# A batched 64 x 64 matmul: block diagonals cleared by GpSimd, first b tiles on two queues, third a tile turned later

## The chip, the cores and the metric

The kernel runs on one core of one Trainium2 chip. A core has a matrix engine (TensorE, PE in the profile), a vector engine (VectorE, DVE), a scalar engine (ScalarE, ACT), GpSimd (POOL) and SyncE (SP). Each takes its own instructions in the order in which they were written and waits on semaphores for the others. Transfers between the chip's memory (HBM) and the on-chip memory (SBUF) are issued from SP, ACT or POOL, and carried out by 16 DMA engines. PE writes its products to PSUM, and another engine copies them to SBUF. The metric is the time of one execution in microseconds. A difference of 2% is about what a measurement of this kernel can tell from no change.

## What is computed

```python
def setup_inputs():
    return {
        "a": np.random.randn(1024, 64, 64).astype(np.float32),
        "b": np.random.randn(1024, 64, 64).astype(np.float32),
    }

def reference(a, b):
    return np.matmul(a, b).astype(np.float32)
```

There are 1024 independent products of 64 x 64 matrices. Each input has 16.8 MB and so has the output: 50.3 MB in all cross between HBM and SBUF.

## The kernel before

**Tiles.** A tile t is 64 products (16 tiles, `n_t`), and a step s is two tiles (8 steps, `n_s`). b is the moving operand of the matmul. a has to be turned first, since PE wants it with the inner dimension on the partitions. Four turned matrices are then laid on the diagonal of a 128-row operand that is zero elsewhere: the block diagonal, `at_bd0` and `at_bd1`, used in turn by even and odd tiles. Both are cleared once, at the start, one by DVE and one by GpSimd; later tiles write over the same diagonal places. Everything is computed in bf16. Two bf16 numbers are often moved as one fp32 word.

**Loads of a.** A step of a comes in four quarters h of 0.5 MB. The first step (`load_first_a`) is loaded as fp32, two quarters on SP's queue and two on ACT's, and is cast on ACT. Every later step (`load_a`) is loaded with three quarters cast to bf16 by the transfer itself, on POOL's queue (`cast_load_a`, tile `a_sb`), and the fourth as fp32 on SP's queue (tile `a_raw`). There are three buffers of each.

**Turning a.** Steps 0 and 1 (`ON_DVE`) are turned by DVE, one quarter at a time (`turn_a`), with the quarters that are still fp32 first cast by ACT. From step 2 on, `regroup` copies a step into one bf16 tile on DVE, `transpose` turns it on PE against an identity in two halves j, and ACT copies the results to `at_sb`. In all steps `spread` then copies the pieces to the block diagonal on DVE.

**b.** Tiles 0 to 3, 14 and 15 are loaded as fp32 (`load_b`, 1 MB each; the queue by `FIRST_B`, else SP) and cast by `cast`. Steps 2 to 6 (`PAIRS`) are loaded as a pair of tiles, in four transfers that cast to bf16 on POOL's queue (`load_pair`), and put in order by DVE (`turn`, one half per tile). All share three buffers (`b_sb`): a load waits until what was in its buffer has been cast or turned.

**Products.** `multiply` runs 64 matmuls per tile, in two halves with a PSUM tile `o_ps` each (two buffers). `evacuate` copies each half to `o_sb` in four copies, on ACT; in later odd tiles DVE does two of the second half's four. The result is stored one tile later (`HOLD`), in one transfer of 1 MB on POOL's queue; tile 14 goes in two, and tile 15 in four quarters on ACT's and SP's queues.

**Order.** The schedule is written by hand (`tc.manual_schedule()`): each engine runs its instructions in the order of the loop over t. In round t, `spread` and `cast` prepare tile t+1, `multiply` does tile t, then come the turning of later steps and the store of tile t-1. POOL's queue therefore mixes loads and stores in a fixed order, and each transfer on it waits for the one eight places earlier to be complete. For the start that order is a1, a2 (three casts each), the pair of step 2, a3, a4, the pair of step 3, the store of tile 0. The last load in it is a7, behind the store of tile 4.

The lines that matter: memsets 268 and 269, first loads 97, 105 and 76, casts 151, 154 and 197, DVE's turning of a 160, spreads 173 (steps 0 and 1) and 183, regroup 126 and 129, PE's transposes 138 with copies 141, pairs 111 and their turning 120, matmuls 241, evacuation 229, stores 218.

Of the kernel before, what the change touches and what calls it, by code (L numbers as in the profile page):

```python
# [8 lines left out]
fp32 = mybir.dt.float32  # L9
bf16 = mybir.dt.bfloat16  # L10
# [3 lines left out]
def kernel(  # L14
# [14 lines left out]
    nc = tc.nc  # L29
# [4 lines left out]
    n_t, n_s = B // 64, B // 128  # L34
    A_AHEAD = 3
# [2 lines left out]
    HOLD = 2  # L38
    PAIRS = (2, 3, 4, 5, 6)
    ON_DVE = (0, 1)  # L40
    FIRST_B = {0: nc.sync, 1: nc.sync, 2: nc.scalar, 3: nc.scalar}

    a_v = a.rearrange("(s g h) (mp v) k -> s h g mp (v k)", h=4, g=32, v=16)
    bp_v = b.rearrange("(s g h) k n -> s h g (k n)", h=4, g=32)
# [35 lines left out]

    def load_a(s, a_sb=None):
        a_sb = a_sb or cast_load_a(s)
        a_raw = a_pool.tile([128, 16, 64], fp32, name="a_raw")
        nc.sync.dma_start(out=a_raw[:].rearrange("p v k -> p (v k)"), in_=a_v[s, 3])
        a_tiles[s] = a_sb, a_raw

    def load_first_a():
# [34 lines left out]
    def regroup(s):  # L122
        a_sb = a_tiles.pop(s)
        a_bf = work.tile([128, 16, 4, 64], bf16, name="a_bf")
        cast_sb, raw = a_sb
        nc.vector.tensor_copy(  # L126
            a_bf[:, :, 0:3, :], cast_sb[:].rearrange("p h v k -> p v h k")
        )
        nc.vector.tensor_copy(a_bf[:, :, 3, :], raw[:])  # L129
        abf_tiles[s] = a_bf  # L130
        at_tiles[s] = work.tile([128, 32, 4, 4, 4], fp32, name="at_sb")

# [13 lines left out]
    def turn_a(s, h):  # L146
        if s == 0:
            if h == 0:
                abf_tiles[0] = work.tile([128, 16, 4, 64], bf16, name="a_bf")
            rows = abf_tiles[0][:, 4 * h : 4 * h + 4]  # L150
            nc.scalar.copy(rows.rearrange("p x y k -> p (x y k)"), a_tiles[0][h])  # L151
        elif h == 3:
            rows = work.tile([128, 16, 4, 64], bf16, name="a_bf")[:, 0:4]
            nc.scalar.copy(rows.rearrange("p x y k -> p (x y) k"), a_tiles[s][1][:])  # L154
        else:
            rows = a_tiles[s][0][:, h : h + 1]
        if h == 0:
            at_tiles[s] = work.tile([128, 4, 8, 4, 4, 4], fp32, name="at_sb")
        pairs = rows.rearrange("p x y k -> p (x y k)").bitcast(fp32)
        nc.vector.transpose(  # L160
            at_tiles[s][:, h].rearrange("p g w mp vo -> p w vo g mp"),
            pairs.rearrange("p (vo w kp) -> p w vo kp", vo=4, w=4),
        )

    def spread(t, hs=range(4)):
        bd = bd_tiles[t % N_BD]
        at_sb = at_tiles[t // 2]
        for h in hs:
            rows = slice(32 * h, 32 * h + 32)
            if t // 2 in ON_DVE:  # L170
                for i in range(2):
                    block = 32 * (2 * (t % 2) + i)
                    nc.vector.tensor_copy(  # L173
                        bd[rows, 8 * i : 8 * i + 8, :, h, :, :].rearrange(
                            "p g w mp vo -> p (g w) (mp vo)"
                        ),
                        at_sb[block : block + 32, h].rearrange(
                            "p g w mp vo -> p (g w) (mp vo)"
                        ),
                    )  # L180
            else:
                half = slice(16 * (t % 2), 16 * (t % 2) + 16)
                nc.vector.tensor_copy(  # L183
                    bd[rows, :, :, h, :, :].rearrange("p g w mp vo -> p (g w) (mp vo)"),
                    at_sb[rows, half].rearrange("p g w mp vo -> p (g w) (mp vo)"),
                )

    def cast(t):
        s, half = t // 2, t % 2
        if s in PAIRS:  # L190
            return
        if half == 0:
            bbf_tiles[s] = work.tile([128, 32, 128], bf16, name="b_bf")
        b_bf = bbf_tiles[s][:, 16 * half : 16 * half + 16]
        b_sb = b_tiles.pop(t)
        if t < n_t - 1:
            (nc.vector.tensor_copy if t > 1 else nc.scalar.copy)(b_bf, b_sb)  # L197
# [12 lines left out]
    def multiply(t):  # L210
        at_bd = bd_tiles[t % N_BD][:].rearrange("p g (j wl) h mp vo -> p j g (wl h mp vo)", j=2)
        at_bd = at_bd.bitcast(bf16).rearrange("p j g (c u) -> p j g c u", u=2)
        b_bf = bbf_tiles[t // 2][:, 16 * (t % 2) : 16 * (t % 2) + 16]
        last = t == n_t - 1
        o_sb = o_pool.tile([128, 8, 2, 2, 64], fp32, name="o_sb")

        def put(lo, n):
            store_queue(t, lo).dma_start(  # L218
                out=o_v[t, :, lo : lo + n, :],
                in_=o_sb[:, lo : lo + n].rearrange("p gh j wl n -> p (gh j wl n)"),  # L220
            )

        def evacuate(o_ps, gh, n, copies):

            for par in range(2):
                for wl in range(2):
                    src = o_ps[64 * wl : 64 * wl + 64, :, par, :, :]
                    dst = o_sb[64 * par : 64 * par + 64, gh : gh + n, :, wl, :]
                    copies[2 * par + wl](dst, src)  # L229

        for half in range(2):
            if not last:
                o_ps = o_psum.tile([128, 4, 2, 2, 64], fp32, name="o_ps")
            for g8 in range(8):
                if last and g8 % 4 == 0:
                    o_ps = t_psum.tile([128, 2, 2, 2, 64], fp32, name="at_ps")
                g = 8 * half + g8
                gl = (g8 % 4 if last else g8) // 2
                for j in range(2):
                    for u in range(2):  # L240
                        nc.tensor.matmul(  # L241
                            o_ps[:, gl, g % 2, j, :],
                            at_bd[:, j, g, :, u],
                            b_bf[:, g, 64 * u : 64 * u + 64],
                            start=(u == 0),
                            stop=(u == 1),
                        )
                if last and g8 % 4 == 3:
                    copy = nc.scalar.copy if g8 == 3 else nc.vector.tensor_copy
                    evacuate(o_ps, g // 4 * 2, 2, [copy] * 4)  # L250
            if not last:
                copies = [nc.scalar.copy] * 4
                if half and t % 2 and t > 6:
                    copies[2:] = [nc.vector.tensor_copy] * 2
                evacuate(o_ps, 4 * half, 4, copies)
        if last:
            held[t] = [lambda q=q: put(2 * q, 2) for q in range(4)]
        else:
            whole = t < n_t - 2
            held[t] = [lambda q=q: put(q, 8 if whole else 4) for q in ([0] if whole else [0, 4])]  # L260

    with tc.manual_schedule():
# [2 lines left out]
        nc.scalar.copy(warm[:, 1:2], warm[:, 0:1])  # L265
        load_b(0)
        load_b(1)
        nc.vector.memset(bd_tiles[0][:], 0.0)  # L268
        nc.gpsimd.memset(bd_tiles[1][:], 0.0)
        load_a(1)  # L270
        load_a(2)
        make_identity(nc, identity)
        for h in range(4):
            turn_a(0, h)
            spread(0, [h])
        cast(0)
        load_b(2)
        for t in range(n_t):
            s, half = t // 2, t % 2
            if t + 1 < n_t:  # L280
                spread(t + 1)
                cast(t + 1)
            if t == 0:
                load_b(3)
                load_pair(2)
            if t in (1, 2):
                load_pair(t + 2)
            if t in (8, 10):
                load_b(14 + (t - 8) // 2)
            if half == 0 and 0 < s < n_s - 1 - A_AHEAD:  # L290
                load_a(s + 1 + A_AHEAD)
            if half == 0 and 0 < s < n_s - 1:
                transpose(s + 1, 1)
            multiply(t)
            if t == 0:
                for h in range(4):
                    turn_a(1, h)
                a_tiles.pop(1)
                load_a(A_AHEAD)
                load_a(A_AHEAD + 1)  # L300
            if s + 1 in PAIRS:
                turn(s + 1, half)
                if half and 4 < s + 4 <= max(PAIRS):
                    load_pair(s + 4)
            if t == 1:
                regroup(2)
                transpose(2, 0)
            elif half == 0 and 0 < s and s + 2 < n_s:
                regroup(s + 2)
            elif half == 1 and s + 2 < n_s:  # L310
                transpose(s + 2, 0)
            if t >= HOLD - 1:
                store(t - HOLD + 1)
        for t in range(n_t - HOLD + 1, n_t):
# [31 lines left out]
```

## Time and profile before

| | us |
|---|---|
| median of 3 runs | 137.26 |
| lowest, highest | 135.27, 137.62 |
| the profiled execution | 136.3 |
| its span (first to last instruction) | 134.5 |

| engine | busy us | share of the span |
|---|---|---|
| DVE | 103.1 | 77% |
| ACT | 92.0 | 68% |
| PE | 66.9 | 50% |
| POOL | 46.0 | 34% |

| queue | MB written | share of 16 DMA engines |
|---|---|---|
| POOL's (q0) | 26.48 | 71.8% |
| SP's (q1) | 9.44 | 20.0% |
| ACT's (q10) | 3.67 | 8.0% |

The first numbers come from separate runs; everything else comes from the one profiled execution. Bytes of a queue are counted where they are written, so a load that casts to bf16 counts half of the fp32 that it reads. Line numbers are those of the kernel before; with the change the same functions stand some lines further down.

### The profile page before, as it was taken

What the parts mean: (1) busy time and instruction counts of PE and PEld (TensorE: products, weight loads), DVE (VectorE), ACT (ScalarE), POOL (GpSimd) and SP (SyncE); (2) the same over time, 40 slices, a digit from 0 to 9 for tenths busy, and PEclk for the clock granted to TensorE, in tenths of its full rate; (3) what the DMA queues carried; (4) which work ended last, traced back from release to release, by engine and by line L of the source; (5) the groups of instructions that cost most, each with busy time, mean ns of one, the idle gap of its engine ahead of it and who ended that gap; (6) DMA issues with size and microseconds to landing.
All of it is one profiled execution on the core that took longest, in us unless ns stands there. A gap on an engine that the chain in (4) does not pass through costs nothing.

```text
span 134.5 us, 2765 instructions
## 1 busy us (share of the span) xinstructions
PE 66.9 (50%) x1120; PEld 64.3 (48%) x1120; DVE 103.1 (77%) x133; ACT 92.0 (68%) x157; POOL 46.0 (34%) x64
## 2 busy tenths in 40 slices
PE   0000054055059667259936657674767475876400
PEld 0000054055059656259926657574757375866400
DVE  5699991006998999999998599989929999396900
ACT  3453140999715899999999909991898449999600
POOL 8940000391432374435345425363220020435000
PEclk9999999999999999965896777777775775555685
DMA  3999999999999999999999999999999999999991
GB/s 72 385 334 272 270 271 336 357 353 228 221 285 252 241 232 275 359 218 224 297 339 212 344 242 347 251 299 350 256 374 398 398 407 397 370 331 308 333 330 56
DMA packets 13932, 39.76 MB, mean 296 GB/s; under 512 B 1248, under 2 KB 2272, under 8 KB 13280
## 3 DMA queue, kind: packets, MB, share of 16 engines
q0 software_dynamic: 8080, 26.48, 71.8%
q1 hardware_dynamic: 3952, 9.44, 20.0%
q10 hardware_dynamic: 1888, 3.67, 8.0%
q8 instruction: 9, 0.15, 0.4%
q14 instruction: 3, 0.02, 0.0%
HBM read 33.55 MB, written 16.78 MB: 374 GB/s over the span
## 4 chain that ended last, share of the span: by engine, by line
DMA 65%; DVE 10%; ACT 7%; issue 5%; POOL 2%; PE 2%; SPq 2%; DVEq 0%; POOLq 0%
DMA b_sb<-in_b_dram 24%; DMA a_sb<-in_a_dram 23%; DMA out_dram<-o_sb 19%; ACT o_sb L229 5%; DVE at_bd L183 4%; DVE o_sb L229 4%; DVE b_bf L120 2%; POOL b_sb L111 1%; ACT b_bf L197 1%; PE at_ps L241 1%; SPq L105 1%; SPq L97 1%; PE o_ps L241 1%; POOL out_dram L218 0%; POOL a_sb L76 0%
## 5 line engine op out<-in xcount | busy, mean ns | idle before, releaser
L229 ACT COPY o_sb<-o_ps 64x512 f32<-64x512 f32 x112 | 65.0, 580 | 12.8 <-PE o_ps L241 11.2
L241 PEld LDWEIGHTS <-at_bd 128*128 128x128 bf16 x1024 | 47.9, 118 | 54.0 <-issue 36.2
L241 PE MATMUL o_ps<-b_bf,at_bd 128*128 128x64 bf16 x960 | 46.7, 222 | 50.7 <-ACT o_sb L229 22.6
L183 DVE COPY at_bd<-at_sb 32x1024 f32<-32x1024 f32 x48 | 34.2, 713 | 1.2
L218 POOL DMA_DIRECT2D out_dram<-o_sb x16 | 15.8, 990 | 36.5 <-issue 7.2
L120 DVE STREAM_TRANSPOSE b_bf<-b_sb 128x1024 f32<-128x1024 f32 x10 | 22.1, 2213 | 0.4 <-DMA b_sb<-in_b_dram 0.2
L138 PE MATMUL at_ps<-identity,a_bf 128*128 128x128 f32 x96 | 18.5, 374 | 7.2 <-DVE a_bf L129 7.2
L111 POOL DMA_DIRECT2D b_sb<-in_b_dram x20 | 12.0, 602 | 28.3 <-ACT b_bf L197 17.5
L138 PEld LDWEIGHTS at_ps<-identity,a_bf 128*128 128x128 f32 x96 | 16.9, 202 | 7.5 <-issue 6.6
L76 POOL DMA_DIRECT2D a_sb<-in_a_dram x21 | 14.0, 689 | 13.2 <-DMA b_sb<-in_b_dram 7.5
L141 ACT COPY at_sb<-at_ps 128x512 f32<-128x512 f32 x24 | 12.9, 596 | 5.6 <-PE at_ps L138 5.3
L160 DVE STREAM_TRANSPOSE at_sb<-a_bf 128x512 f32<-128x512 f32 x5 | 5.3, 1055 | 11.8 <-ACT a_bf L154 10.5
L173 DVE COPY at_bd<-at_sb 32x512 f32<-32x512 f32 x32 | 13.5, 423 | 0.7
L197 ACT CAST b_bf<-b_sb 128x2048 bf16<-128x2048 f32 x2 | 3.8, 1897 | 10.6 <-DMA b_sb<-in_b_dram 10.6
L229 DVE COPY o_sb<-o_ps 64x512 f32<-64x512 f32 x8 | 5.5, 689 | 4.8 <-ACT o_sb L229 4.7
L126 DVE COPY a_bf<-a_sb 128x3072 bf16<-128x3072 bf16 x6 | 5.8, 966 | 2.4 <-DMA a_sb<-in_a_dram 2.4
L151 ACT CAST a_bf<-o_sb 128x1024 bf16<-128x1024 f32 x4 | 4.1, 1044 | 3.2 <-DMA o_sb<-in_a_dram 3.2
L129 DVE CAST a_bf<-a_raw 128x1024 bf16<-128x1024 f32 x6 | 4.5, 746 | 0.0
L229 DVE COPY o_sb<-at_ps 64x256 f32<-64x256 f32 x8 | 3.4, 422 | 1.2 <-PE at_ps L241 1.1
L241 PE MATMUL at_ps<-b_bf,at_bd 128*128 128x64 bf16 x64 | 3.6, 242 | 1.2 <-DVE at_bd L183 1.2
L268 DVE MEMSET at_bd<- 128x4096 f32 x1 | 3.5, 3472 | 0.8 <-issue 0.8
L197 DVE CAST b_bf<-b_sb 128x2048 bf16<-128x2048 f32 x3 | 3.7, 1227 | 0.4 <-DMA b_sb<-in_b_dram 0.3
(16 smaller groups left out, 15.0 us busy)
## 6 DMA issues: line engine op xcount, KB each, us to landing
out_dram<-o_sb POOLq DMA_DIRECT2D x14, 1024.0 KB, 14.1
a_sb<-in_a_dram POOLq DMA_DIRECT2D x21, 256.0 KB, 13.6
b_sb<-in_b_dram POOLq DMA_DIRECT2D x20, 256.0 KB, 12.3
a_raw<-in_a_dram SPq DMA_DIRECT2D x7, 512.0 KB, 9.4
o_sb<-in_a_dram SPq DMA_DIRECT2D x2, 512.0 KB, 6.1
o_sb<-in_a_dram ACTq DMA_DIRECT2D x2, 512.0 KB, 6.9
out_dram<-o_sb POOLq DMA_DIRECT2D x2, 512.0 KB, 7.1
out_dram<-o_sb ACTq DMA_DIRECT2D x2, 256.0 KB, 6.3
```

Of the source, the lines that this page charges most:

```text
L76: nc.gpsimd.dma_start(out=a_sb[:, h, :, :].rearrange("p v k -> p (v k)"), in_=a_v[s, h], single_packet=True)
L111: nc.gpsimd.dma_start(out=pair[32 * h : 32 * h + 32, 0], in_=bp_v[s, h])
L120: nc.vector.transpose(cols[:, u], rows[:, u])
L126: nc.vector.tensor_copy(a_bf[:, :, 0:3, :], cast_sb[:].rearrange("p h v k -> p v h k"))
L138: nc.tensor.transpose(at_ps[:, vo, :], a_cols[:, 4 * vo + 2 * j + wl, :], identity[:])
L141: nc.scalar.copy(at_tiles[s][:, :, 2 * j + wl, :, :], at_ps[:].rearrange("p vo (g mp) -> p g mp vo", mp=4),)
L173: nc.vector.tensor_copy(bd[rows, 8 * i : 8 * i + 8, :, h, :, :].rearrange("p g w mp vo -> p (g w) (mp vo)"), at_sb[block : block + 32, h]. ...
L183: nc.vector.tensor_copy(bd[rows, :, :, h, :, :].rearrange("p g w mp vo -> p (g w) (mp vo)"), at_sb[rows, half].rearrange("p g w mp vo -> p ...
L197: (nc.vector.tensor_copy if t > 1 else nc.scalar.copy)(b_bf, b_sb)
L218: store_queue(t, lo).dma_start(out=o_v[t, :, lo : lo + n, :], in_=o_sb[:, lo : lo + n].rearrange("p gh j wl n -> p (gh j wl n)"),)
L229: copies[2 * par + wl](dst, src)
L241: nc.tensor.matmul(o_ps[:, gl, g % 2, j, :], at_bd[:, j, g, :, u], b_bf[:, g, 64 * u : 64 * u + 64], start=(u == 0), stop=(u == 1),)
```

## The change

The second memset moves from DVE to GpSimd, and both, with the identity, stand ahead of GpSimd's first load. b0 stays first on SP's queue, b1 moves to ACT's right behind ACT's two quarters of a0, and b2 moves up behind b0 on SP's. b3 comes on SP's queue, after cast 0, in place of ACT's after cast 1. The fourth quarter of a1 is loaded with a cast on POOL's queue, so ACT no longer casts it. Of ACT's work in the head, the cast of a0's first quarter and half of cast 0 go to DVE; of DVE's, the spread of quarter 2 of tile 0 goes to ACT. On POOL's queue a3 and a4 are loaded in rounds 0 and 1, which puts a4 behind the pair of step 3; the pair of step 5 comes one round earlier, ahead of the store of tile 1. Step 2 of a is turned on PE behind the matmuls of tile 2 (before: both halves ahead of them), and both halves of the pair of step 2 are put in order in round 2 (before: rounds 2 and 3); step 3 is regrouped in round 3 (before: round 2). DVE takes half of the second half's evacuation in tiles 12 and 14 too.

```diff
-    FIRST_B = {0: nc.sync, 1: nc.sync, 2: nc.scalar, 3: nc.scalar}
+    FIRST_B = {1: nc.scalar}
...
     def load_a(s, a_sb=None):
         a_sb = a_sb or cast_load_a(s)
-        a_raw = a_pool.tile([128, 16, 64], fp32, name="a_raw")
-        nc.sync.dma_start(out=a_raw[:].rearrange("p v k -> p (v k)"), in_=a_v[s, 3])
+        a_raw = a_pool.tile([128, 16, 64], fp32, name="a_raw")[:].rearrange("p v k -> p (v k)")
+        if s in ON_DVE:
+            a_raw = a_raw.bitcast(bf16)[:, 0:1024]
+            nc.gpsimd.dma_start(out=a_raw, in_=a_v[s, 3], single_packet=True)
+        else:
+            nc.sync.dma_start(out=a_raw, in_=a_v[s, 3])
         a_tiles[s] = a_sb, a_raw
...
-            rows = abf_tiles[0][:, 4 * h : 4 * h + 4]
-            nc.scalar.copy(rows.rearrange("p x y k -> p (x y k)"), a_tiles[0][h])
+            rows = abf_tiles[0][:, 4 * h : 4 * h + 4].rearrange("p x y k -> p (x y k)")
+            (nc.scalar.copy if h else nc.vector.tensor_copy)(rows, a_tiles[0][h])
         elif h == 3:
-            rows = work.tile([128, 16, 4, 64], bf16, name="a_bf")[:, 0:4]
-            nc.scalar.copy(rows.rearrange("p x y k -> p (x y) k"), a_tiles[s][1][:])
+            rows = a_tiles[s][1]
...
-    def spread(t, hs=range(4)):
+    def spread(t, hs=range(4), copy=nc.vector.tensor_copy):
...
-        if t < n_t - 1:
+        if t == 0:
+            nc.scalar.copy(b_bf[:, 0:8], b_sb[:, 0:8])
+            nc.vector.tensor_copy(b_bf[:, 8:16], b_sb[:, 8:16])
+        elif t < n_t - 1:
             (nc.vector.tensor_copy if t > 1 else nc.scalar.copy)(b_bf, b_sb)
...
-                if half and t % 2 and t > 6:
+                if half and (t % 2 and t > 6 or t > 11):
                     copies[2:] = [nc.vector.tensor_copy] * 2
...
         load_b(0)
         load_b(1)
-        nc.vector.memset(bd_tiles[0][:], 0.0)
-        nc.gpsimd.memset(bd_tiles[1][:], 0.0)
+        load_b(2)
+        for bd in bd_tiles:
+            nc.gpsimd.memset(bd[:], 0.0)
+        make_identity(nc, identity)
         load_a(1)
         load_a(2)
-        make_identity(nc, identity)
-        for h in range(4):
-            turn_a(0, h)
-            spread(0, [h])
+        turn_a(0, 0)
+        spread(0, [0])
+        turn_a(0, 1)
+        spread(0, [1])
+        turn_a(0, 2)
+        turn_a(0, 3)
+        spread(0, [2], nc.scalar.copy)
+        spread(0, [3])
         cast(0)
-        load_b(2)
+        load_b(3)
         for t in range(n_t):
...
-            if t == 0:
-                load_b(3)
-                load_pair(2)
-            if t in (1, 2):
+            if t < 3:
                 load_pair(t + 2)
+                load_a(t + A_AHEAD) if t < 2 else None
...
-            if half == 0 and 0 < s < n_s - 1:
+            if half == 0 and 1 < s < n_s - 1:
                 transpose(s + 1, 1)
             multiply(t)
             if t == 0:
                 for h in range(4):
                     turn_a(1, h)
                 a_tiles.pop(1)
-                load_a(A_AHEAD)
-                load_a(A_AHEAD + 1)
-            if s + 1 in PAIRS:
-                turn(s + 1, half)
-                if half and 4 < s + 4 <= max(PAIRS):
-                    load_pair(s + 4)
-            if t == 1:
+            elif t == 1:
                 regroup(2)
+            elif t == 2:
                 transpose(2, 0)
-            elif half == 0 and 0 < s and s + 2 < n_s:
-                regroup(s + 2)
-            elif half == 1 and s + 2 < n_s:
-                transpose(s + 2, 0)
+                transpose(2, 1)
+                turn(2, 0)
+                turn(2, 1)
+                load_pair(5)
+            elif t == 3:
+                regroup(3)
+                transpose(3, 0)
+            else:
+                if s + 1 in PAIRS:
+                    turn(s + 1, half)
+                    if half and s + 4 <= max(PAIRS):
+                        load_pair(s + 4)
+                if half == 0 and s + 2 < n_s:
+                    regroup(s + 2)
+                elif half == 1 and s + 2 < n_s:
+                    transpose(s + 2, 0)
             if t >= HOLD - 1:
                 store(t - HOLD + 1)
```

More of the change, by code (lines that the diff above doesn't have):

```diff
@@ L128, in regroup @@
         )
-        nc.vector.tensor_copy(a_bf[:, :, 3, :], raw[:])
+        nc.vector.tensor_copy(a_bf[:, :, 3, :], raw.rearrange("p (v k) -> p v k", v=16))
         abf_tiles[s] = a_bf
@@ L149, in turn_a @@
                 abf_tiles[0] = work.tile([128, 16, 4, 64], bf16, name="a_bf")
-            rows = abf_tiles[0][:, 4 * h : 4 * h + 4]
-            nc.scalar.copy(rows.rearrange("p x y k -> p (x y k)"), a_tiles[0][h])
+            rows = abf_tiles[0][:, 4 * h : 4 * h + 4].rearrange("p x y k -> p (x y k)")
+            (nc.scalar.copy if h else nc.vector.tensor_copy)(rows, a_tiles[0][h])
         elif h == 3:
-            rows = work.tile([128, 16, 4, 64], bf16, name="a_bf")[:, 0:4]
-            nc.scalar.copy(rows.rearrange("p x y k -> p (x y) k"), a_tiles[s][1][:])
+            rows = a_tiles[s][1]
         else:
-            rows = a_tiles[s][0][:, h : h + 1]
+            rows = a_tiles[s][0][:, h].rearrange("p v k -> p (v k)")
         if h == 0:
             at_tiles[s] = work.tile([128, 4, 8, 4, 4, 4], fp32, name="at_sb")
-        pairs = rows.rearrange("p x y k -> p (x y k)").bitcast(fp32)
+        pairs = rows.bitcast(fp32)
         nc.vector.transpose(
@@ L172, in spread @@
                     block = 32 * (2 * (t % 2) + i)
-                    nc.vector.tensor_copy(
+                    copy(
                         bd[rows, 8 * i : 8 * i + 8, :, h, :, :].rearrange(
```

## The prediction

> **What bounds the kernel now.** First the page's DMA row and its HBM line.
>
> ```profile
> DMA  3999999999999999999999999999999999999991
> HBM read 33.55 MB, written 16.78 MB: 374 GB/s over the span
> ```
>
> The transfer engines are busy from 3 us to the end, while no compute engine passes 77%. The change moves the same 50.33 MB. So I ask at what rate they cross, by stretch, and then what the last stores wait for. The windows give the rate (start:end, length, the engines' busy times, granted clock, DMA share, GB/s):
>
> ```profile
> 4.00:8.00 4.00, 0.00 (x0) 0.00 (x0) 2.72 (x3) 2.09 (x2) 3.92 (x9) 1.00 1.03 416
> 8.00:20.00 12.00, 1.74 (x34) 1.85 (x35) 11.56 (x22) 3.89 (x4) 0.23 (x1) 1.00 1.09 273
> 20.00:28.00 8.00, 1.93 (x38) 1.82 (x36) 0.83 (x1) 4.34 (x7) 2.23 (x5) 1.00 1.05 348
> 28.00:40.00 12.00, 5.00 (x71) 4.75 (x71) 8.37 (x16) 8.11 (x14) 5.30 (x8) 1.00 1.05 264
> 100.00:115.00 15.00, 10.26 (x153) 9.76 (x151) 14.40 (x18) 10.66 (x19) 1.97 (x3) 0.61 1.03 399
> 115.00:130.00 15.00, 8.41 (x149) 7.85 (x146) 9.02 (x17) 11.29 (x23) 4.17 (x4) 0.61 0.97 332
> ```
>
> GB/s counts bytes written; a load that casts fp32 to bf16 reads twice that. By the queue table of the same stretches POOL's queue (casts only, until 40 us) wrote 1.51 MB in 8 to 20, 0.06 in 20 to 28 and 1.35 in 28 to 40. With these doubled, HBM moved 398, 355 and 375 GB/s there. Full pace is about 400, and it is missed in two places: 20 to 40 us moved 7.34 MB where 8.0 could pass (1.65 us lost), and 115 to 130 us 4.95 where 6.0 could (2.6 us).
>
> The timeline of the head (start, length, engine, line; in brackets the idle time before and what ended it):
>
> ```profile
> 16.31 1.90 ACT L197 CAST b_bf<-b_sb 128x2048 bf16<-128x2048 f32 x1 [5.20 <-DMA b_sb<-in_b_dram]
> 18.26 3.57 PE L241 MATMUL o_ps<-b_bf,at_bd 128*128 128x64 bf16 x64 [18.26 <-ACT b_bf L197]
> 23.58 1.90 ACT L197 CAST b_bf<-b_sb 128x2048 bf16<-128x2048 f32 x1 [5.37 <-DMA b_sb<-in_b_dram]
> 25.77 2.00 POOL L111 DMA_DIRECT2D b_sb<-in_b_dram  x4 [17.54 <-ACT b_bf L197]
> ```
>
> Tile 0's multiplication waits for b0 (landed 16.3), and POOL stands still for 17.5 us until b1 is cast and its buffer free. That hole is the slow stretch: in 20 to 28 us only SP's and ACT's queues move bytes.
>
> The timeline of the tail:
>
> ```profile
> 100.18 1.13 DVE L126 COPY a_bf<-a_sb 128x3072 bf16<-128x3072 bf16 x1 [2.40 <-DMA a_sb<-in_a_dram]
> ...
> 114.21 1.23 DVE L197 CAST b_bf<-b_sb 128x2048 bf16<-128x2048 f32 x1
> ...
> 117.78 1.39 DVE L229 COPY o_sb<-o_ps 64x512 f32<-64x512 f32 x2 [2.34 <-ACT o_sb L229]
> ...
> 119.20 3.09 DVE L183 COPY at_bd<-at_sb 32x1024 f32<-32x1024 f32 x4
> ...
> 122.34 3.44 PEld L241 LDWEIGHTS <-at_bd 128*128 128x128 bf16 x64 [1.33 <-DVE at_bd L183]
> ```
>
> From the landing of the last a tile (a7) at 100.1 us the work runs through DVE in its issue order: regroup, spread 12, evacuation of 11, turn of b, spreads 13 and 14, cast 14, evacuation of 13, spread 15, tile 15. DVE ends at 127.8 and the last stores land some 5 us later. So the end is set by (a) when a7 lands, which is a matter of bytes ahead of it, and (b) the chain behind it.
>
> **The change, part by part.**
>
> *GpSimd.* The second memset (3.51, row L269) and the identity (0.30 + 0.35) go ahead of POOL's loads: the first issue moves from 4.19 to 8.35 us. In before nothing of that queue moved until after 8 us, 4 us behind its issue, so I expect its first bytes near 12.5. Cover: the a0 loads (2.1 MB) and b0, b1, b2 (1.05 MB each) are on SP and ACT by then, 5.2 MB or 13 us at 400 GB/s from 2.4 us on. Cost 0; without the cover up to 4.2 us. a1's fourth quarter becomes a POOL cast, one issue more (0.57) ahead of pair 2: the seven end at 12.3, before cast 1 (about 17) lets pair 2 go.
>
> *DVE and ACT in the head.* DVE loses its memset (3.47), which lay beside the wait for a0. One cast of a0 goes from ACT (1.04) to DVE (nearest row L129, 0.75). Two spreads go from DVE (0.42) to ACT, unseen there: between 0.58 (row L229, 512 elements) and 1.04 (row L151, 1024 from SBUF), I take 0.65. All of it is beside the wait for b0. Cast 0 is halved between both engines: 1.90 becomes 1.0.
>
> *b on both queues.* b0 leads SP's queue, b1 leads ACT's right behind a0, b2 follows on SP. a0, b0 and b1 are 4.2 MB, 10.5 us at 400: b0 and b1 land near 14 to 14.5 (16.3 and 23.6 before). Multiplication 0 starts near 15.5 (18.3), cast 1 ends near 17, pair 2 is issued then (25.8), and POOL's queue has no hole. a1 needs no ACT cast, so DVE's 10.5 us wait for it goes: a1 is turned by about 24 (32.3). b2 lands near 21, multiplication 2 starts near 28.5, no longer queued on PE behind the transposes of a2 (42.0 before). b3 is now on SP, behind b2 and the raw quarter of a2 and ahead of the raw quarter of a3: beside pair loads that queue had 0.73 MB in 28 to 40, so b3 lands at 36 (42.3 at worst, as before). Four tiles are ahead by 8 to 13 us, and then DVE, busy 19.13 of 20 us in 40 to 60, absorbs most: multiplication 4 waits for spread 4, regroup 3 and the transposes of a3, near 50 (52.6).
>
> *What of it reaches the end.* a7 is the last load in POOL's order, with the same five stores ahead of it as before. Its landing moves only by the better rate. If the hole is gone, 20 to 40 us gains between 0 and 1.65 us. The early stretch of b0 beside b1 on the two queues resembles the 355 row, and could give back 5 us x 45 GB/s = 0.23 MB, 0.55 us. I take half of the gain, 0.8.
>
> *Tail.* Evacuation of the second halves of tiles 12 and 14 moves half to DVE: four ACT copies less (4 x 0.58), four DVE copies more (4 x 0.69 = 2.76). In DVE's order from 106.1: turn 2.2, spread 13 2.8, two copies 1.4 (new), spread 14 2.85, cast 14 1.23: 116.6. There DVE used to wait 2.34 us for ACT's evacuation of tile 13, up to 117.78. ACT has two copies less ahead of it, and o_ps is free earlier, so DVE goes straight on: copies to 118.0, spread 15 to 121.0 (122.3 before), cast 15 0.83, two copies (new) 1.4 to 123.2, while PE starts tile 15 at once. DVE's last copy ends near 126.6 in place of 127.8: 1.15 us. DMA has room in 115 to 130.
>
> Sum: 0.8 + 1.15 = 1.95. The profiled execution took 136.3 us (span 134.5 and 1.8 around it): 134.35. The median shown is 137.26, 0.96 above it; I put the forecast between, at 134.8.
>
> **Rivals.** *No change, 136.0 to 137.3.* The head is hidden whole, because bytes bound it. First, 0.63 MB of b15 still crossed after a7 (SP's queue in 100 to 115); issued earlier and ahead of a7 they delay it by 1.6 us, which leaves 0.35 of the sum. Second, the rate may not depend on which queues are filled: the rows of 398 and 355 differ in the kinds of packets too; then the 0.8 goes and the sum is 135.15. Third, DVE's early copies may not run beside GpSimd's longer memsets: two spreads beside the identity's took 1.00 where 0.85 is usual. If the first cast waits from 5.3 to 7.8, 2.4 us of the 2.6 us lead at tile 4 are gone. Against all three: DVE's 2.34 us wait in the tail is real.
>
> The Trainium skill (DMA: Bandwidth & Descriptors, section "Issuing engines are not separate DMA queues") states the second as a rule: all issuing engines' DMAs run on the same 16 engines, and spreading them saves only issue time. The Trainium skill (SBUF — State Buffer, section "Who interferes with whom") states the third: a DVE copy in a two-port mode and a GpSimd instruction exclude each other for a whole instruction. The rows before the change agree with both, and prove neither.
>
> *Both losses recovered, 132.1.* 1.65 + 2.6 = 4.2 us off 136.3. For: in 120 to 125 us the DMA share is 0.91, so the stores come late. Against: the chain behind a7 shortens by 1.15 only.
>
> *Slower, 139 to 141.* DVE becomes the tail's bound. Its 2.76 us of new copies wait in order, and pay nothing back where PE's second half of tile 12 or 14 isn't ready: each such wait holds spread 14 or the last copies. It decides once DVE's idle 2.34 us is gone, which the first two copies and one wait of 1 us use up; then all 2.76 stand at the end, 139.1, or 140.0 on the median, and more with waits. For: DVE is 14.40 of 15 us busy in 100 to 115. Against: PE ends tile 12 by 111, when spread 13 ends.
>
> **How the numbers follow.** Forecast 0.45 (own range 133.3 to 136), no change 0.22, both recovered 0.17, slower 0.16. Two per cent of the median, 2.75 us, is about what runs that spread from 135.27 to 137.62 can tell: under 134.5 is faster, over 140 slower. Half of the forecast's case and all of the third are faster: 0.39. Two thirds of the slower case pass 140: 0.11. The rest is 0.50. The range leaves out the far side of the last two cases: 132 to 138.8.
>
> **What would show it.** Right: PE's first multiplication at 15 to 16.5 us, pair 2 issued near 17, and no stretch under 390 GB/s of HBM traffic between 20 and 40. a7's landing at 98 to 100; DVE going from cast 14 to the copies of tile 13 with under 0.5 us between; its last copy 1 us or more closer to that landing than 27.7. Wrong: the same a7 landing with a filled hole (bytes, the second case); DVE's last copy later behind a7 (the fourth); or slow DMA between 8 and 13 us, with GpSimd's loads late and no cover.

## The result and the profile after

The changed kernel takes 137.61 us (median of 20 runs, 136.40 to 138.86) beside 136.15 (20 runs, 135.12 to 137.62) for the kernel before on the same chip: a ratio of 1.0109, 95% interval 1.0079 to 1.0138. It is slower by 1.1%. With 20 runs of each kernel the interval reaches 0.3% to either side, so differences well under the 2% named at the start can be told. The prediction was 134.8 with a range of 132.0 to 138.8: the range holds the time, the sign is wrong. The profiled execution took 137.22 us, with a span of 135.4 (before 136.3 and 134.5).

The page of the changed kernel, its DMA row and its HBM line:

```profile
DMA  3999999999999999999999999999999999984993
HBM read 33.55 MB, written 16.78 MB: 372 GB/s over the span
```

The hole is now near the end: a slice at 40%, where before every slice but the first and the last was full. The windows of the changed kernel (start:end, length, busy time of PE, PEld, DVE, ACT and POOL, granted clock, DMA share, GB/s written):

```profile
8.00:16.00 8.00, 0.00 (x0) 0.10 (x1) 7.07 (x11) 3.22 (x4) 4.65 (x8) 1.00 1.06 299
...
100.00:115.00 15.00, 8.13 (x112) 7.74 (x112) 11.67 (x15) 7.24 (x13) 0.89 (x1) 0.66 1.03 394
115.00:130.00 15.00, 9.06 (x160) 8.61 (x160) 14.46 (x24) 9.98 (x21) 4.23 (x4) 0.55 0.83 286
120.00:124.00 4.00, 3.47 (x64) 3.31 (x63) 3.86 (x6) 2.16 (x4) 1.36 (x1) 0.50 0.47 170
```

The last of these stretches, in the kernel before:

```profile
120.00:124.00 4.00, 2.83 (x55) 2.67 (x53) 3.06 (x5) 3.86 (x8) 2.36 (x3) 0.50 0.89 314
```

In 120 to 124 us the transfer engines have half of their time free (a share of 0.47, before 0.89): the stores come too late to fill it. That is the tail. The head shows in the queues of 8 to 16 us (packets, MB written, share of 16 engines), in the changed kernel:

```profile
q10 hardware_dynamic: 536, 1.09, 45.2%
q1 hardware_dynamic: 530, 1.05, 44.8%
q0 software_dynamic: 122, 0.25, 16.4%
```

and in the kernel before:

```profile
q0 software_dynamic: 536, 1.00, 65.9%
q1 hardware_dynamic: 563, 1.12, 40.4%
q10 hardware_dynamic: 34, 0.07, 2.4%
```

With POOL's casts (q0) counted twice, as they read twice what they write, HBM moved 1.09 + 1.05 + 0.50 = 2.64 MB in these 8 us, or 330 GB/s, beside 1.12 + 0.07 + 2.00 = 3.19 MB, or 399, before. In both the engines are occupied all the time (the shares add up to more than 100%). In 20 to 40 us it is the other way: 5.46 MB written, of which 2.68 by casts, make 8.14 MB or 407 GB/s, where 7.34 MB moved before. So the slow stretch was not filled but moved, from 20-40 us to 8-16. What is left over is small: by the packets of the trace 14.40 MB had crossed at 40 us, beside 14.12 before, 0.28 MB or 0.7 us at 400 GB/s.

Nothing of that shows at a7, whose regroup starts at 100.63 us (100.18 before). In 100 to 116 us SP's queue carried 0.31 MB, beside 0.63 before: 0.32 MB more of b15 had crossed ahead of a7. In all, 39.1 MB had crossed when a7 was there, 38.7 before.

Behind a7, DVE's timeline in the changed kernel:

```profile
108.47 3.16 DVE L186 COPY at_bd<-at_sb 32x1024 f32<-32x1024 f32 x4
114.05 1.39 DVE L235 COPY o_sb<-o_ps 64x512 f32<-64x512 f32 x2 [2.42 <-ACT o_sb L235]
115.47 3.09 DVE L186 COPY at_bd<-at_sb 32x1024 f32<-32x1024 f32 x4
118.59 1.23 DVE L203 CAST b_bf<-b_sb 128x2048 bf16<-128x2048 f32 x1
119.85 1.39 DVE L235 COPY o_sb<-o_ps 64x512 f32<-64x512 f32 x2
121.28 3.09 DVE L186 COPY at_bd<-at_sb 32x1024 f32<-32x1024 f32 x4
```

Spread 13 ends at 111.63, 11.0 us behind the start of the last regroup, as before. Then DVE waits 2.42 us for ACT, and only after that come the two new copies of tile 12 (114.05) and spread 14 (115.47). The wait of 2.34 us that stood behind cast 14 is gone, as forecast, but one of 2.42 us now stands ahead of the new copies. DVE waits for ACT as long as before, so the copies that were to fill this wait come on top of it: counted from the start of the last regroup, spread 14 ends 3.9 us later than before and spread 15 still 1.6 us later. PE's timeline in the changed kernel, and the start of tile 14 in the kernel before:

```profile
112.87 1.09 PE L247 MATMUL o_ps<-b_bf,at_bd 128*128 128x64 bf16 x32 [0.94 <-ACT o_sb L235]
115.59 1.87 PE L247 MATMUL o_ps<-b_bf,at_bd 128*128 128x64 bf16 x32 [1.62 <-DVE o_sb L235]
119.88 3.59 PE L247 MATMUL o_ps<-b_bf,at_bd 128*128 128x64 bf16 x64 [2.42 <-DVE b_bf L203]
```

```profile
116.60 1.87 PE L241 MATMUL o_ps<-b_bf,at_bd 128*128 128x64 bf16 x32 [0.51 <-ACT o_sb L229]
```

Of the changed kernel, the first two rows are the halves of tile 13, the third is tile 14. Its start is 3.3 us later than before, and the second half of tile 13 waits 1.62 us for DVE's new copies to free `o_ps`. DVE's last copy ends 29.75 us behind the start of the last regroup, 27.58 before. The last transfer ends at 133.92, 0.83 later than before (133.09): of the 2.2 us in the chain more than half is taken back, for the last store is through 3.5 us behind DVE's last copy, where it took 5.3. That the emptier queues are the reason was not tested.

### The profile page after: what moved, and what is told of

The parts are those of the page before. It is cut to its first block, busy times and chain, and to the rows that moved or that the text cites. A ratio compares the mean times of both kernels' runs of the same rounds, so it can differ in the third digit from the quotient of the medians.

```text
span 135.4 us, 2775 instructions
## 1 busy us (share of the span) xinstructions
PE 65.2 (48%) x1120; PEld 62.2 (46%) x1120; DVE 106.0 (78%) x136; ACT 88.0 (65%) x152; POOL 49.2 (36%) x66
## 4 chain that ended last, share of the span: by engine, by line
DMA 63%; DVE 13%; issue 6%; POOL 6%; PE 5%; ACT 2%; DVEq 0%; POOLq 0%
DMA b_sb<-in_b_dram 28%; DMA a_sb<-in_a_dram 23%; DMA out_dram<-o_sb 11%; DVE o_sb L235 5%; PE o_ps L247 5%; DVE at_bd L186 4%; POOL at_bd L276 3%; ACT o_sb L235 2%; POOL a_sb L76 2%; DVE b_bf L124 2%; DVE b_bf L203 1%; DVE b_bf L208 1%; DVE a_bf L133 1%; POOL identity masks.py:199 0%; POOL a_raw L86 0%
## 5 line engine op out<-in xcount | busy, mean ns | idle before, releaser
L235 ACT COPY o_sb<-o_ps 64x512 f32<-64x512 f32 x108 | 62.7, 580 | 21.0 <-PE o_ps L247 19.6
L142 PE MATMUL at_ps<-identity,a_bf 128*128 128x128 f32 x96 | 16.6, 345 | 10.1 <-DVE a_bf L133 10.1
L76 POOL DMA_DIRECT2D a_sb<-in_a_dram x21 | 13.4, 645 | 18.4 <-DMA a_sb<-in_a_dram 12.2
L142 PEld LDWEIGHTS at_ps<-identity,a_bf 128*128 128x128 f32 x96 | 15.0, 184 | 10.3 <-issue 6.0
L176 DVE COPY at_bd<-at_sb 32x512 f32<-32x512 f32 x30 | 12.7, 423 | 0.8
L235 DVE COPY o_sb<-o_ps 64x512 f32<-64x512 f32 x12 | 8.3, 690 | 4.3 <-ACT o_sb L235 4.2
L276 POOL MEMSET at_bd<- 128x4096 f32 x2 | 7.0, 3512 | 0.3 <-POOLq L347 0.3
L155 DVE CAST a_bf<-o_sb 128x1024 bf16<-128x1024 f32 x1 | 3.4, 3418 | 4.1 <-DMA o_sb<-in_a_dram 4.1
L155 ACT CAST a_bf<-o_sb 128x1024 bf16<-128x1024 f32 x3 | 3.0, 1043 | 3.7 <-DMA o_sb<-in_a_dram 3.7
L163 DVE STREAM_TRANSPOSE at_sb<-a_bf 128x512 f32<-128x512 f32 x4 | 4.0, 1045 | 0.1
```

The costliest lines, as they stand in the source:

```text
L76: nc.gpsimd.dma_start(out=a_sb[:, h, :, :].rearrange("p v k -> p (v k)"), in_=a_v[s, h], single_packet=True)
L142: nc.tensor.transpose(at_ps[:, vo, :], a_cols[:, 4 * vo + 2 * j + wl, :], identity[:])
L155: (nc.scalar.copy if h else nc.vector.tensor_copy)(rows, a_tiles[0][h])
L176: copy(bd[rows, 8 * i : 8 * i + 8, :, h, :, :].rearrange("p g w mp vo -> p (g w) (mp vo)"), at_sb[block : block + 32, h].rearrange("p g w ...
L276: nc.gpsimd.memset(bd[:], 0.0)
```

## The experiments

Two causes stand against each other. **Head theory:** both memsets and the identity ahead of POOL's first load leave 8 to 16 us without casts, and bytes not moved there are paid for at the end. **Tail theory:** the copies of tiles 12 and 14 given to DVE wait for ACT and hold spread 14 up. All ratios are to the kernel before on the same chip; every row of the table is from one profiled execution except the ratio. These columns vary: e5 and e16 are the same kernel, and their last regroups start at 100.01 and 97.75. Small differences between two traces therefore say little.

| kernel | ratio, 95% interval | last regroup starts | DVE's last copy ends | last transfer ends |
|---|---|---|---|---|
| before | 1 | 100.18 | 127.76 | 133.09 |
| the change | 1.0109 [1.0079, 1.0138] | 100.63 | 130.38 | 133.92 |
| e1 tail undone | 1.0019 [0.9988, 1.0049] | 101.22 | 128.67 | 133.03 |
| e2 tail alone | 1.0042 [1.0010, 1.0075] | 101.00 | 130.27 | 133.96 |
| e3 tile 14 only | 1.0061 [1.0022, 1.0099] | 100.91 | 129.41 | 133.40 |
| e4 tile 12 only | 1.0171 [1.0134, 1.0208] | 101.69 | 130.82 | 135.09 |
| e5 e1, memsets split | 0.9942 [0.9908, 0.9977] | 100.01 | 128.19 | 132.56 |
| e6 e1, b1 on SP | 1.0023 [0.9985, 1.0061] | 100.73 | 128.92 | 133.28 |
| e8 DVE's copies first | 1.0069 [1.0028, 1.0110] | 101.02 | 129.23 | 133.21 |
| e10 e5, b14, b15 on POOL | 0.9959 [0.9911, 1.0008] | 96.27 | 124.77 | 131.47 |
| e12 change, memsets split | 0.9958 [0.9920, 0.9996] | 98.76 | 128.54 | 132.42 |

**e1 and e2: the tail rule, taken out and put in alone.** e1 is the change without it, e2 the kernel before with it.

```diff
-                if half and (t % 2 and t > 6 or t > 11):
+                if half and t % 2 and t > 6:
```

> The changed kernel with the evacuation of tiles 12 and 14 as it was before (all four copies of the second half on ACT); the head stays changed. Tail theory: in the changed kernel DVE stood 2.42 us for ACT's first copies of tile 12 before its own two, with spread 14 queued behind them, so DVE ended 29.8 us behind a7's landing where 27.7 was usual. Without the rule it ends 27.7 us behind a landing near 100.5, and the time is that of the kernel before: ratio 0.998 to 1.003. Rival, head theory (slow transfers in 8 to 16 us and late GpSimd loads cost the time): the ratio stays 1.008 to 1.014.

> The kernel before with only the new evacuation rule for tiles 12 and 14. Tail theory: DVE stands about 2.4 us ahead of its copies of tile 12, ends 2 us later behind a7, and the ratio is 1.009 to 1.016. Head theory: no change, 0.998 to 1.002.

Without the rule the change's loss falls from 1.1% to an interval that holds 1: 0.9% belong to the rule. Alone, on the old head, it costs 0.4%. That is less than the 0.9 to 1.6% expected, although DVE's wait (1.96 us) and the longer chain (29.3 us from the last regroup to DVE's last copy) are there too; so what the rule costs depends on the rest of the kernel. DVE's timeline in e1:

```profile
109.06 6.02 DVE L186 COPY at_bd<-at_sb 32x1024 f32<-32x1024 f32 x8
115.11 1.23 DVE L203 CAST b_bf<-b_sb 128x2048 bf16<-128x2048 f32 x1
118.68 1.39 DVE L235 COPY o_sb<-o_ps 64x512 f32<-64x512 f32 x2 [2.35 <-ACT o_sb L235]
```

Spreads 13 and 14 stand in one piece again and end at 115.1, where the change ends them at 118.6; the wait for ACT is back behind cast 14, ahead of spread 15 alone. e1 also shows that the change's head alone, with all that it reorders, gains nothing measurable (1.0019, the interval holds 1).

**e3 and e4: one tile of the rule at a time.**

```diff
-                if half and (t % 2 and t > 6 or t > 11):
+                if half and (t % 2 and t > 6 or t > 13):    (e3)
+                if half and (t % 2 and t > 6 or t == 12):   (e4)
```

> The changed kernel with the new evacuation for tile 14 alone. Tail theory: no wait ahead of spread 14; the two copies of tile 14 stand ahead of DVE's last eight, which wait for tile 15's matmuls anyway, so they cost 0.6 us at most: ratio 1.000 to 1.006. If the cost were DVE's added busy time (4 copies of 0.69) and no wait, half of it would stay: 1.005 to 1.008. Head theory: 1.008 to 1.014.

> The changed kernel with the new evacuation for tile 12 alone. Tail theory: the wait of 2.4 us ahead of DVE's copies stays, and nearly the whole loss with it: ratio 1.006 to 1.012. Busy-time theory: half of the loss, 1.004 to 1.007. Head theory: 1.008 to 1.014.

Tile 12 is the costly one, as the place of the wait says. The ratio of e3 (1.0061) lies at the end of the range of its tail theory and inside that of the busy-time theory, so it does not decide between them. That tile 12 alone cost more than both tiles together (1.0171 beside 1.0109, the intervals just touching, with five timed runs) was not foreseen, and no run settles it. In its one trace the chain is not the longer one (29.1 us behind the last regroup, 29.75 in the change); the regroup itself starts 1.1 us later.

**e8: the same copies, but the first two of a half in place of the last two.**

```diff
-                if half and (t % 2 and t > 6 or t > 11):
+                if half and t % 2 and t > 6:
                     copies[2:] = [nc.vector.tensor_copy] * 2
+                if half and t in (12, 14):
+                    copies[:2] = [nc.vector.tensor_copy] * 2
```

> The changed kernel, with DVE doing the first two copies of the second half in tiles 12 and 14, and ACT the last two. Same number of copies on each engine. If DVE's wait of 2.42 us is for ACT's copies of the same tile, it shrinks to the end of PE's second half (0.3 to 0.6 us), spread 14 comes 2 us sooner and the ratio is 1.001 to 1.006. If the copies cost by their busy time alone, nothing changes: 1.008 to 1.014.

This tells whether DVE had waited for PE or for ACT. DVE's timeline in e8:

```profile
112.57 1.39 DVE L235 COPY o_sb<-o_ps 64x512 f32<-64x512 f32 x2 [0.55 <-PE o_ps L247]
113.99 3.09 DVE L186 COPY at_bd<-at_sb 32x1024 f32<-32x1024 f32 x4
```

And who kept ACT waiting in the same kernel (releaser, us, times), from the view of the tile `o_sb`:

```profile
  PE o_ps L247: 17.0, 8
  DVE o_sb L235: 4.0, 2
```

DVE's wait falls from 2.42 to 0.55 us, and now PE ends it. Spread 14 starts 1.5 us earlier than in the change. In exchange ACT waits 4.0 us for DVE, in two waits, for which the change's trace has no such entry: the four copies of one half run one engine after the other in this program, whichever comes first. So DVE's wait in the change was for ACT's two copies of the same half, which end there at 114.02, and not for the product. The time (1.0069) lies between the change and e1, in neither of the two ranges expected, and its interval overlaps the change's: the trace decides this, not the time.

**e5 and e12: the memsets split again.** DVE clears one block diagonal and POOL the other, POOL's casts are issued right behind that, and the identity comes after them. e5 has the old tail rule, e12 the change's.

```diff
-        for bd in bd_tiles:
-            nc.gpsimd.memset(bd[:], 0.0)
-        make_identity(nc, identity)
+        nc.vector.memset(bd_tiles[0][:], 0.0)
+        nc.gpsimd.memset(bd_tiles[1][:], 0.0)
         load_a(1)
         load_a(2)
+        make_identity(nc, identity)
```

> The changed kernel with the old evacuation rule (as e1_tail_undone), and with the clearing shared again: DVE clears the first block diagonal, GpSimd the second, and GpSimd's loads go ahead of the identity. Cover theory: without casts in flight the loads of b0 and b1 run at 315 to 345 GB/s in 8 to 16 us, where 400 is usual; with the casts 4.2 us earlier these 8 us move 0.5 MB more, DVE's first cast takes 0.7 us in place of 3.42, and the ratio falls from 1.002 to 0.988 to 0.996. Rival (what is gained in the head goes to loads of b that cross ahead of a7, and the end doesn't move): 0.998 to 1.004.

> The whole change, evacuation of tiles 12 and 14 included, with the clearing alone shared between DVE and GpSimd as before, and GpSimd's loads ahead of the identity. If the two costs add (1.0109 with both; 1.0019 without the tail; 0.9942 without either), this is 1.001 to 1.006. If one hides the other, it stays at 1.008 to 1.013 or falls under 0.998.

With the old rule the ratio goes from 1.0019 to 0.9942, with the change's from 1.0109 to 0.9958. Everything else of the head is untouched, so 0.8 to 1.5% belong to these lines: one memset back on DVE, and the identity behind POOL's casts. Which of the two matters more was not tried; both let POOL's first issue come at 4.19 us again, not 8.48. e12 also came out under 0.998, where the sum of the two costs would have given 1.001 to 1.006: they do not simply add.

The gain can be followed to a7. At 40 us, 14.03 to 14.12 MB have crossed in the traces with the old head, 14.32 to 14.40 with the change's and 14.78 to 14.97 with the mended one (the memsets split). In the eight traces in which POOL clears both block diagonals (the change, e1, e3, e4, e6, e8, e13, e14), the last packet of a7 comes at 100.1 to 101.2 us; in the four with the memsets split and b as in the change (e5, e12, e15, e16) and in e9, the same up to there, at 97.3 to 99.5; in the three with the old head (before, e2, e7) at 99.7 to 100.9. So the change's head does not bring a7 forward, and the mended one does.

**e6: b1 on SP's queue behind b0, not on ACT's.**

```diff
-    FIRST_B = {1: nc.scalar}
+    FIRST_B = {}
```

> The changed kernel with the old evacuation rule (as e1_tail_undone), and b1 on SP's queue behind b0, so that ACT's queue is empty after a0. If the slow 8 to 16 us come from two queues of b's 512-byte pieces side by side, HBM moves over 380 GB/s there with one queue; if they come from the missing casts, it stays at 315 to 345. b1 lands some 4 us later. Ratio 0.998 to 1.006 by either, for the end follows a7.

The rival for the slow 8 to 16 us is that two queues of b disturb each other. The queues of that stretch in e6:

```profile
q1 hardware_dynamic: 975, 1.96, 83.7%
q0 software_dynamic: 168, 0.31, 20.5%
q10 hardware_dynamic: 30, 0.07, 2.1%
```

They move 1.96 + 0.07 + 0.62 = 2.65 MB, or 331 GB/s: the change's 330 with one queue of b in place of two. What is missing is the casts. That they are what restores the rate shows in the same kernel as e5, profiled once more (e16 below), which has them there:

```profile
q0 software_dynamic: 401, 0.76, 49.9%
q1 hardware_dynamic: 416, 0.85, 30.6%
q10 hardware_dynamic: 412, 0.84, 27.1%
```

That is 3.21 MB, or 401 GB/s, with b on both queues. The rival falls. The two rates hold in every trace: 326 to 331 GB/s where POOL clears both block diagonals, 399 to 404 in all others. Why b's loads move less without casts beside them stays open.

**e7 and e9: the wait for a7 filled.** DVE idles before the last regroup (4.53 us in the change). In e7 (from the kernel before) the last step's regroup and transposes go behind the products of tile 12; in e9 (from e5) the regroup goes into round 11 and the transposes behind the products of tile 12. The lines added in e9 (in e7 all three calls stand under t == 12; the lines that leave step 7 out of the old places are not shown):

```diff
+                if t == 11:
+                    regroup(7)
+                elif t == 12:
+                    transpose(7, 0)
+                    transpose(7, 1)
```

> The kernel before, with regroup and transposes of step 7 moved behind the matmuls of tile 12, so that spread 12, the evacuation of tile 11, the turn of b and spread 13 no longer stand in DVE's order behind the wait for a7. Chain theory (the end follows a7's landing and the DVE work behind it): the wait of 2.4 to 5 us is filled, DVE ends 25 to 25.5 us behind a7 in place of 27.6, ratio 0.983 to 0.990. Byte theory (the transfers alone set the end): 0.996 to 1.002, with the transfer engines no less busy in 116 to 124 us than before.

> e5_memset_split, with step 7's regroup moved in DVE's order behind spread 12, the evacuation of tile 11 and the turn of b, and its transposes behind the matmuls of tile 12. Chain theory: DVE uses its 3.7 us wait for a7, and since the transposes come out by 112 to 113, spread 14 starts 1 us or more sooner than in e5; ratio 0.984 to 0.991. Byte theory (the transfers set the end, as the late regroup of e7 suggested): 0.993 to 0.999, as e5.

1.0023 [0.9986, 1.0061] and 0.9994 [0.9949, 1.0039]: no gain over their bases. DVE's timeline in e7 has the reason:

```profile
114.48 2.83 DVE L183 COPY at_bd<-at_sb 32x1024 f32<-32x1024 f32 x4 [4.38 <-ACT at_sb L141]
```

and in e9:

```profile
114.50 2.83 DVE L186 COPY at_bd<-at_sb 32x1024 f32<-32x1024 f32 x4 [4.24 <-ACT at_sb L145]
```

The wait for a7 became one of over 4.2 us for ACT's copies of a7's transposes, ahead of spread 14, and the end stays.

**e10 and e11: b14 and b15 behind a7.** POOL's queue keeps its order, so there they cross after a7 and no longer delay it. e10 is e5 with this, e11 has e9's edit too.

```diff
-    FIRST_B = {1: nc.scalar}
+    FIRST_B = {1: nc.scalar, 14: nc.gpsimd, 15: nc.gpsimd}
```

> e5_memset_split, with b14 and b15 issued on GpSimd's queue, where they come behind a7 in order. If a7's landing is set by the bytes ahead of it, 1.5 MB less cross ahead of it and it lands 3 to 3.7 us earlier, near 97. Chain theory: the end follows, as far as the stores can: ratio 0.978 to 0.988. Byte theory: the same bytes have to cross in all, ratio 0.992 to 0.999; and if b15 lands too late for its casts, over 1.

> e9 and e10 together. Chain theory: both gains add in part, ratio 0.975 to 0.985. Byte theory: 0.992 to 0.999.

The last packet of a7 comes at 94.6 us in e10 and at 94.5 in e11, where the five traces with the same head and b14 and b15 on SP's queue have 97.3 to 99.5. This shows that the bytes of b ahead of a7 delay its landing. DVE ends 3.4 us earlier than in e5, but the last transfer only 1.1 (and 0.4 later than in e16's trace of e5's kernel), and the ratio (0.9959) is not below e5's. The windows of e10 show what ends it:

```profile
116.00:128.00 12.00, 5.46 (x96) 5.17 (x96) 7.38 (x15) 7.40 (x16) 3.27 (x3) 0.50 1.01 359
```

The transfer engines are full up to 128 us, while DVE's last copy ends at 124.77: now bytes bound the end, not the chain. e11 came to 0.9983 [0.9941, 1.0025], no better than either edit alone.

**e13 to e16: the four corners on one chip.** The change, e1, e12 and e5 once more.

> The four corners once more, on one chip: head as in the change or with the memsets split and the first two casts ahead of the identity, tail rule as in the change or as before. This is the change itself: both theories 1.010 to 1.012 of before (1.011 so far).

> The change's head with the tail rule of before. Both theories 1.002 of before: 0.9% under the change, since tile 12's copies no longer hold spread 14 up.

> Head mended, tail rule of the change. Additive theory (the tail rule costs its 0.9% whatever the head does): e16's ratio plus 0.009, so 1.003. Interacting theory (with 0.8 MB more across by 44 us the last transfers bound the end and the tail rule's wait is partly covered): within 0.003 of e16's ratio, so 0.994 to 0.997.

> Head mended, tail rule of before. Both theories 0.994 of before. If it is 0.998 or more, the head's repair is not a gain over the kernel before and only undoes the change's loss.

| ratio, 95% interval | tail rule of the change | tail rule of before |
|---|---|---|
| POOL clears both first | 1.0122 [1.0074, 1.0171] | 1.0035 [0.9999, 1.0071] |
| memsets split, casts first | 0.9959 [0.9923, 0.9995] | 0.9918 [0.9882, 0.9953] |

The first three repeat their first values within 0.2%, the fourth is 0.2% lower. The memsets' order is worth 1.6% with the change's tail rule and 1.2% with the old one, and in neither column do the intervals overlap: this is shown. The rule costs 0.9% on the change's head, as before. On the repaired head the difference is 0.4%, between the 0.9% of the additive theory and the 0.3% of the interacting one, and the intervals overlap, so how much of the rule's cost remains there is open. The lower right corner beats both kernels: 0.8% faster than before, and 2% faster than the change.

## Why the prediction was wrong

**What bounds the kernel** was read rightly: the bytes' rate in the head, and a chain behind a7. The two slow stretches, 20-40 and 115-130 us, are where the change acted. Of the sum, 0.8 us in the head and 1.15 in the tail, neither came: by e1 the head is worth nothing, and by e1 beside the change the tail's rule costs 0.9%, 1.2 us. That the range holds 137.61 is no merit of the mechanism, for the time lies above the forecast's own range (to 136) and the "no change" case (to 137.3). All three signs of being wrong that the prediction named came: a7 where it was although the hole was filled, DVE's last copy later behind it, and slow transfers between 8 and 13 us (303 GB/s by the packets) with POOL's loads late.

**Head, POOL's loads.** The prediction moved POOL's first issue to 8.35 us (8.48 came) and its first bytes to 12.5 (13.6 came, by the packets of the trace). It set the cost at 0 because 5.2 MB on the other queues cover the gap. They did keep the engines occupied, but at 330 GB/s, not 400. The cover was reckoned at 400 GB/s and should have been reckoned at the rate of those bytes. The prediction allowed for this with 0.55 us to give back; by the packets, 4.68 MB had crossed at 16 us beside 5.20, a loss of 0.52 MB or 1.3 us at 400 GB/s. e5 and e12 show that undoing it makes the change a gain. POOL's timeline in the changed kernel:

```profile
8.48 1.78 POOL L76 DMA_DIRECT2D a_sb<-in_a_dram  x3
...
19.61 2.19 POOL L115 DMA_DIRECT2D b_sb<-in_b_dram  x4 [6.96 <-ACT b_bf L203]
```

and its first loads in the kernel before:

```profile
4.19 3.40 POOL L76 DMA_DIRECT2D a_sb<-in_a_dram  x6
```

**Head, the hole in 20-40 us** was filled as forecast: pair 2 was issued at 19.61 (25.77 before, about 17 forecast), and none of the five stretches of 4 us between 20 and 40 moved under 393 GB/s. From 16 to 40 us 0.80 MB more crossed than before, 2.0 us at 400 GB/s. Net of the loss that is 0.7 us, close to the 0.8 taken, but by luck: the gain was larger than the 1.65 reckoned at most, and the loss more than twice the 0.55.

**From there to a7** the prediction let the 0.8 through to its landing. The "no change" rival's first mechanism took it: in these two traces 0.32 MB more of b15 crossed ahead of a7, 0.8 us at 400 GB/s. e10 bears the rival's mechanism out: with b14 and b15 behind it, a7 lands earlier. Its size is not shown: behind a7's last packet 0.69 MB of b15 were left in the kernel before and 0.30 in the change, but 0.37 and 0.34 in e2 and e7, which have the old head too.

**The early steps.** PE's first product came at 17.57, not 15 to 16.5, with b0's cast waiting for bytes. It proved no sign of the time: in e16, the fastest, it starts at 20.19. DVE's first cast came out as the third mechanism had it. The timelines of DVE and POOL in the changed kernel:

```profile
4.97 3.42 DVE L155 CAST a_bf<-o_sb 128x1024 bf16<-128x1024 f32 x1 [4.09 <-DMA o_sb<-in_a_dram]
...
0.74 6.96 POOL L276 MEMSET at_bd<- 128x4096 f32 x2 [0.29 <-POOLq L347]
```

and DVE's in e16:

```profile
1.70 3.47 DVE L275 MEMSET at_bd<- 128x4096 f32 x1 [0.83 <-issue]
5.12 0.83 DVE L155 CAST a_bf<-o_sb 128x1024 bf16<-128x1024 f32 x1
```

The same cast takes 3.42 us beside POOL's memset, which ends at 7.70, and 0.83 without one; it ends 0.69 behind the memset, as if it had run from there. It cost nothing, for the turned a0 was spread by 15.4 and b0's cast began at 16.48. The Trainium skill (SBUF — State Buffer, section "Who interferes with whom") says that a DVE copy or cast in a two-port mode and a GpSimd instruction share a pair of ports that one of them holds for a whole instruction, while the other is blocked; the trace agrees with 3.42 beside 0.83 us.

The second mechanism, that the rate does not depend on which queues are filled, is half right. By e6, one queue or two of b make no difference: 331 and 330 GB/s. The Trainium skill (DMA: Bandwidth & Descriptors, section "Issuing engines are not separate DMA queues") says that DMAs started by different engines run on the same 16 DMA engines, and that starting them on several saves only issue time; these rows agree. But the rate does depend on whether casts are among the transfers: 330 without, 401 with them.

**Tail: the step that failed.** The prediction's order of DVE ran "turn 2.2, spread 13 2.8, two copies 1.4 (new), spread 14 2.85, cast 14 1.23: 116.6". It put the two new copies right behind spread 13 with no wait, since PE's tile 12 would be done, and let them use up the 2.34 us that DVE waited behind cast 14. PE was done at about 111.9; ACT's two copies of the same half were not, until 114.02. DVE waited 2.42 us ahead of the copies, and cast 14 ended at 119.82. "o_ps is free earlier" failed with it: it came free later (PE's 1.62 us wait for DVE). The 1.15 us of gain became 2.2 us of loss in the chain, and by e1 0.9% of the time. The "slower" rival had the right mechanism, copies that wait in DVE's order and hold spread 14, but named PE as the one waited for, and so argued it away with PE's end at 111. It also overstated the price (139 us and more), as it let all of the new copies' time, and the waits, reach the end.

"DVE going from cast 14 to the copies of tile 13 with under 0.5 us between" came true (119.82 to 119.85) and proved nothing: the wait had moved to the copies of tile 12, where it was not looked for.

## What to carry to other kernels

When an instruction is put into an in-order engine, ask for each of its operands who else writes or reads that tile, not only who produces the value, and look at what is queued behind it: work put into an engine's idle time costs nothing only if the wait shrinks by it. Here the wait of 2.4 us moved ahead of the new work, and the work came on top. Cover by other transfers has to be reckoned at the rate of those transfers; engines that were busy all the time moved 18% less here (330 for 400 GB/s). And a gain in the head must be followed in bytes to the last load: here other loads took its place.

## What was not expected of the hardware

The b loads on SP's and ACT's queues are slower per packet by themselves than beside casts. From the rows above (share times 16 engines times 8 us, by packets): 0.452 x 128 us / 536 = 108 ns in the change and 110 ns in e6 (0.837 x 128 / 975), beside 94 and 84 ns in e16, where casts fill half of the engines' time, and 92 in the kernel before. Why was not tried.

GpSimd's first bytes came 5.2 us behind the first issue in the change (8.48 to 13.64), and 4.0 in the kernel before (4.19 to 8.19). In these kernels the first load from POOL has this lead, and work put ahead of its issue delayed its first bytes by 5.45 us where the issue moved by 4.29. Why was not tried.
